# A chunk of attention probabilities turned by DMA instead of TensorE, with all engines in one recorded order

## The chip, the cores and the metric

The kernel runs on 1 core of one Trainium2 chip. The metric is the device time of one execution in microseconds (us). Before the change the median of 3 runs is 3124.31 us (3117.63 to 3127.85).

## What is computed

A decoder trunk of two layers on 2048 tokens of width 1024: a Mamba-2 mixer, then multi-head latent attention with 16 heads, and a final norm. The change lies in the attention between the projections, which is this part of the reference:

```python
MLA_HEADS, QK_NOPE, QK_ROPE, V_HEAD, SEQ, Q_BLOCK = 16, 64, 32, 64, 2048, 128

def causal_block_attention(q_nope, q_rope, k_nope, k_rope, v):
    scale = (QK_NOPE + QK_ROPE) ** -0.5
    for i in range(S // Q_BLOCK):
        q0 = i * Q_BLOCK
        kv_len = q0 + Q_BLOCK
        s = einsum('bqhd,bkhd->bhqk', q_nope[:, q0:kv_len], k_nope[:, :kv_len]) + \
            einsum('bqhr,bkr->bhqk', q_rope[:, q0:kv_len], k_rope[:, :kv_len])
        s = s.astype(float32) * scale
        mask = (q0 + local)[:, None] >= arange(kv_len)[None, :]
        p = softmax(where(mask, s, -inf), axis=-1)
        outs.append(einsum('bhqk,bkhd->bqhd', p, v[:, :kv_len]))
```

## The kernel before

Everything up to the per-head queries, keys and values (the Mamba layer, the norms and projections) and everything after the attention (gate, output projection, final norm) is the same in both kernels. Precision is kept by pairs of float16 halves: a product of two such numbers is three matmuls (lines 86, 87 and 88 in `mm3`), and a float32 tile is split by ScalarE, which writes the high half (L124), and VectorE, which subtracts it and writes the low half (L125), both in `pair16`.

The attention (`heads`) works through 64 jobs, one for each of 16 heads and 4 query blocks of 512 queries. The query block is called qb, 0 to 3; because of the mask, block qb sees qb + 1 chunks of 512 keys. A job has these steps:

- **Scores.** For each of its four rows j of 128 queries and each piece of keys of up to 512: three matmuls into a PSUM bank (and a mask product, L1257, on the last piece), a maximum over the piece by VectorE (L1258), one over the pieces (L1262), then the exponential by ScalarE (L1269) into a float32 tile `Pr`, of which there are 24. `cuts` keeps pieces at 256 keys or more.
- **Turning.** The product with the values needs the probabilities with keys on the partitions. For each block k of 128 keys, TensorE transposes the four 128x128 float32 pieces (L1282) into a PSUM bank `tr`, and `pair16` splits the bank into the float16 tile `PTs`. A job has 4 qb + 4 such units, a head 40 with 136 transposes, as the last four units of a job lie on the diagonal and are narrower.
- **Values.** Two matmuls for each unit (L1292, L1293) add to the job's output bank. After the last unit `finish` copies it out (`Os`, L1299); SyncE's queue stores its upper half to `o_d` and GpSimd's queue adds the lower half to the same place (L1305), which waits for that store to land. After a head's last job the sums of the probabilities are turned and stored (L1308 to L1315).

The order of TensorE's work is written by hand: `LAG`, `DEPTH` and `CREDIT` say after which score piece how many units are turned (T) or multiplied (V). The other engines are ordered by the framework's scheduler. The scores own four PSUM banks (`mm`), turned units and outputs four (`tr`). The next head's queries, keys and values are loaded by GpSimd's queue (L1184 to L1198).

Of the kernel before, what the change touches and what calls it, by code (L numbers as in the profile page):

```python
# [20 lines left out]
P = 128  # L21
# [15 lines left out]
NP = 24  # L37
# [3 lines left out]
LAG = 20  # L41
DEPTH = 2
CREDIT = (
    (("VT",), ("TV",), ("VT",), ("TV",)),
    (("", "VTVT"), ("", "TTVV"), ("", "TTVV"), ("", "TTVV")),
    (("TT", "", "VVTV"), ("TV", "", "VTTV"), ("TV", "", "TTVV"), ("TTV", "", "TVV")),
    (("T", "", "", "VVTTVTV"), ("T", "V", "", "VTTVTV"), ("T", "V", "V", "TVTTV"), ("TV", "V", "", "TVTVT")),
)
KV2, CQ2, GA2, ALL2 = 0, 576, 1344, 3392
MAGIC = 12582912.0  # L50
PSCALE = 32768.0
TINY = 2.0 ** -100
# [14 lines left out]
C1, C2, C3 = 6.28125, 1.93500518798828125e-3, 3.01991598196e-7  # L67


class Net:  # L70
# [374 lines left out]
    def constants(self, cp):  # L445
        nc, a = self.nc, self.a
        self.pack = cp.tile([P, PACK], F32, name="pack")
        self.idb = cp.tile([P, P], BF16, name="idb")

        self.un2, self.unh2 = cp.tile([P, 1], F32, name="un2"), cp.tile([P, 1], F32, name="unh2")  # L450

        self.mk = cp.tile([P, 2 * P], BF16, name="mk")
        at = 0
        for name, n in PACKED:
            setattr(self, name, self.pack[:, at:at + n])
            at += n

    def layer_constants(self, cp):
# [13 lines left out]
        nc.vector.memset(self.mk[:, P:], NEG)  # L472
# [24 lines left out]
        nc.vector.tensor_copy(self.mk[:, 0:P], self.mask)  # L497
# [681 lines left out]
    def load_k(self, h, lo, hi):  # L1179

        nc, ts = self.nc, slice(lo * TB, hi * TB)
        if lo == 0:
            self.keys[h] = self.t(self.hp, "K", [96, 2, T], F16, bufs=2)
        nc.gpsimd.dma_start(self.keys[h][0:64, :, ts], self.kn_d[h * 64:(h + 1) * 64, :, ts])  # L1184
        nc.gpsimd.dma_start(self.keys[h][64:96, :, ts], self.kr_d[:, :, ts])

    def load_v(self, h):

        V = self.vals[h] = self.t(self.xq, "xT", [P, T // P, P], F16, bufs=8)
        self.nc.gpsimd.dma_start(V, self.v_d[:, h * P:(h + 1) * P].rearrange("(k p) d -> p k d", p=P))  # L1190

    def load_q(self, h, n):

        nc, ts = self.nc, slice(n * TB, (n + 1) * TB)
        Q = self.quer[h, n] = self.t(self.xq, "xT", [96, 2, TB], F16, bufs=8)
        nc.gpsimd.dma_start(Q[0:64], self.qn_d[h * 64:(h + 1) * 64, :, ts])
        nc.gpsimd.dma_start(Q[64:80], self.q1_d[h * 16:(h + 1) * 16, :, ts])
        nc.gpsimd.dma_start(Q[80:96], self.q2_d[h * 16:(h + 1) * 16, :, ts])  # L1198
# [7 lines left out]
    def attention(self):  # L1206
        with ExitStack() as ctx:
# [3 lines left out]
            with self.tc.manual_schedule(engines={mybir.EngineType.PE}):  # L1211
                self.heads(sp)

    def heads(self, sp):
        nc, v = self.nc, self.nc.vector
        begun = []
        keys, vals, quer = self.keys, self.vals, self.quer

        def cuts(kv):

            out, at = [], 0
            while at < kv:
                w = min(TB, kv - at)
                if kv - at == TB + P:
                    w = 384
                out.append((at, max(w, 256)))
                at += w
            return out

        def scores(h, qb, st):  # L1230

            if h + 1 < NH:
                if qb == 2:
                    self.load_k(h + 1, 0, NB)
                    self.load_v(h + 1)
                self.load_q(h + 1, qb)
            Q, K = quer.pop((h, qb)), keys[h]
            late = []
            for j in range(4):
                qs = slice(j * P, (j + 1) * P)  # L1240
                parts = cuts(qb * TB + (j + 1) * P)
                nb = len(parts)
                nm = self.t(sp, "nm", [P, 1], bufs=4)
                mx = self.t(sp, "mx", [P, 4], bufs=4) if nb > 1 else nm
                banks = []
                for n, (c0, w) in enumerate(parts):
                    if late:
                        late.pop(0)()
                    begun.append(0)
                    s = self.t(self.pp, "tr" if len(begun) <= 18 and len(begun) % 2 == 1 else "mm", [P, TB], bufs=4)  # L1250
                    ks = slice(c0, c0 + w)
                    self.mm3(s[:, :w], Q[:, 0, qs], Q[:, 1, qs], K[:, 0, ks], K[:, 1, ks], True, n < nb - 1)
                    if n == nb - 1:
                        if qb == j == 0:
                            nc.tensor.matmul(s[:, 0:w], self.idb, self.mk, start=False, stop=True)
                        else:
                            nc.tensor.matmul(s[:, w - P:w], self.idb, self.mk[:, 0:P], start=False, stop=True)  # L1257
                    v.tensor_reduce(mx[:, n:n + 1], s[:, :w], AX.X, ALU.max, negate=nb == 1)  # L1258
                    banks.append((s, w))
                    yield CREDIT[qb][j][n]  # L1260
                if nb > 1:
                    v.tensor_reduce(nm, mx[:, :nb], AX.X, ALU.max, negate=True)  # L1262
                p = {}
                st["P"].append(p)

                def exp(n, at=4 * qb + j, parts=parts, banks=banks, nm=nm, p=p):
                    s, w = banks[n]
# [278 lines left out]
```

## Time and profile before

| what | us |
|---|---|
| median of 3 runs | 3124.31 |
| profiled execution, own time | 3126.91 |
| its span, first to last instruction | 3125.1 |
| VectorE (DVE) busy in the span | 2297.6 |
| ScalarE (ACT) busy | 1963.6 |
| GpSimd (POOL) busy | 609.5 |
| DVE's low halves of turned probabilities (L125, PTs) x640 | 373.1 |
| ACT's exponentials (L1269) x631 | 398.7 |
| TensorE's transposes of probabilities (L1282) x2176 | 318.0 |

Durations of one instruction overlap the next one's on the same engine; what an instruction costs in a busy stretch is the distance from its start to the next start. Matmul ends are modelled, so starts are read for TensorE (PE) too. In the lists of groups a row reads: line, engine, operation, tile written and tiles read, shape, count, then busy us, mean ns of one, idle time of the engine before them and what ended it. In a timeline a row has its start and its length in us; x4 at the end means four in a row. In the waits a row reads: who waited for whom, us in total, times, longest.

### The profile page before, as it was taken

How to read it: one execution, taken by the hardware profiler on the slowest of the kernel's cores; microseconds unless marked ns; L12 is line 12 of the kernel's file. 1: busy time of each engine (PE TensorE's matmuls, PEld its weight loads, DVE VectorE, ACT ScalarE, POOL GpSimd, SP SyncE). 2: the span in 40 equal slices, each digit the busy share in tenths (PEclk: the TensorE clock that was granted, in tenths of full speed). 3: DMA queues.
4: the chain of work that ended last, by engine and by line, in shares of the span. 5: the costliest groups of instructions: out<-in, count | busy, mean ns of one | idle time of the engine just before them, and what ended most of it. 6: DMA issues, size and time to landing. Idle time of an engine off the chain costs nothing.

```text
span 3125.1 us, 50616 instructions
## 1 busy us (share of the span) xinstructions
PE 3033.6 (97%) x17815; PEld 1946.3 (62%) x17815; DVE 2297.6 (74%) x4548; ACT 1963.6 (63%) x4952; POOL 609.5 (20%) x855
## 2 busy tenths in 40 slices
PE   8999999999999999999999999999999999999998
PEld 6777754556556665556665455456666666666687
DVE  6878887788776687776755644468888888888676
ACT  7888576665656465654643433368888888888522
POOL 1222022111221112211111212222222222222100
PEclk9999999999999999999999999999999999999999
DMA  5343667655465454754457556632232323233485
GB/s 179 120 135 107 214 201 256 192 157 179 150 220 179 129 161 128 239 192 129 143 159 270 173 163 202 190 96 55 58 64 55 68 53 66 56 73 89 110 270 163
DMA packets 217138, 456.78 MB, mean 146 GB/s; under 512 B 29154, under 2 KB 71138, under 8 KB 215444
## 3 DMA queue, kind: packets, MB, share of 16 engines
q1 hardware_dynamic: 188980, 375.54, 38.2%
q0 software_dynamic: 27904, 78.02, 9.6%
q8 instruction: 140, 2.29, 0.3%
q14 instruction: 114, 0.93, 0.1%
HBM read 332.21 MB, written 121.25 MB: 145 GB/s over the span
## 4 chain that ended last, share of the span: by engine, by line
PE 52%; issue 10%; DVE 9%; ACT 8%; DMA 5%; POOL 3%; SPq 1%; POOLq 0%; ACTq 0%; DVEq 0%
PE mm L86 10%; PE mm L87 10%; PE mm L88 10%; PE tr L1282 7%; PE tr L1292 3%; PE tr L1293 3%; DVE cacc L691 2%; PE tr L86 1%; PE tr L88 1%; PE tr L87 1%; DMA wraw<-in_ssm_w_in_dram 1%; DMA big<-cumT 1%; PE tr L895 1%; ACT Pr L1269 1%; ACT Xw L888 1%
## 5 line engine op out<-in xcount | busy, mean ns | idle before, releaser
L125 DVE SCALAR_TENSOR_TENSOR PTs<-tr,PTs 128x512 f16<-128x512 f32 (+3 forms) x640 | 373.1, 605 | 96.2 <-ACT PTs L124 90.2
L1269 ACT ACTIVATE Pr<-mm,nm 128x512 f32<-128x512 f32 (+2 forms) x631 | 398.7, 642 | 15.0 <-DVE nm L1262 14.2
L124 ACT ACTIVATE PTs<-tr 128x512 f16<-128x512 f32 (+3 forms) x640 | 331.0, 545 | 115.8 <-PE tr L1282 106.8
L1258 DVE TENSOR_REDUCE mx<-mm 128x1 f32<-128x512 f32 (+2 forms) x569 | 336.1, 615 | 21.0 <-PE mm L88 17.7
L1282 PE MATMUL tr<-pack,Pr 128*128 128x128 f32 x2176 | 318.0, 273 | 2.2 <-ACT Os L1299 2.0
L86 PE MATMUL mm<-xT,wsp 128*128 128x512 f16 (+1 forms) x800 | 308.7, 386 | 0.3 <-ACT wsp L116 0.3
L87 PE MATMUL mm<-xT,wsp 128*128 128x512 f16 (+1 forms) x800 | 306.2, 383 | 0.0
L88 PE MATMUL mm<-xT,wsp 128*128 128x512 f16 (+1 forms) x800 | 304.9, 383 | 0.5 <-DVE wsp L117 0.5
L1282 PEld LDWEIGHTS tr<-pack,Pr 128*128 128x128 f32 x2176 | 253.6, 141 | 69.7 <-ACT Os L1299 2.8
L86 PE MATMUL mm<-wsp,xT 128*128 128x512 f16 (+2 forms) x640 | 233.9, 367 | 6.3 <-ACT craw L685 5.1
L691 DVE SCALAR_TENSOR_TENSOR cacc<-craw,pack,cacc 128x512 f32<-128x512 f32 x288 | 217.1, 773 | 28.4 <-ACT cacc L689 26.6
L87 PE MATMUL mm<-wsp,xT 128*128 128x512 f16 (+2 forms) x640 | 233.4, 365 | 1.4 <-DVE wsp L125 1.3
L88 PE MATMUL mm<-wsp,xT 128*128 128x512 f16 (+2 forms) x640 | 233.0, 365 | 0.0
L86 PE MATMUL mm<-K,xT 96*128 96x512 f16 (+2 forms) x639 | 224.0, 350 | 8.2 <-ACT Pr L1269 6.7
L88 PE MATMUL mm<-K,xT 96*128 96x512 f16 (+2 forms) x639 | 223.0, 349 | 0.0
L87 PE MATMUL mm<-K,xT 96*128 96x512 f16 (+2 forms) x639 | 222.4, 348 | 0.0
L1292 PE MATMUL tr<-PTs,xT 128*128 128x512 f16 (+3 forms) x640 | 221.4, 347 | 0.1
L1293 PE MATMUL tr<-PTs,xT 128*128 128x512 f16 (+3 forms) x640 | 219.5, 347 | 0.0
L86 PE MATMUL mm<-wsp,yT 128*128 128x512 f32 x512 | 210.4, 412 | 1.9 <-DVE sz L721 1.3
L87 PEld LDWEIGHTS <-xT 128*128 128x128 f16 (+1 forms) x1280 | 125.5, 98 | 130.8 <-issue 34.8
L844 POOL TENSOR_TENSOR Xp<-Xw,Xp 128x512 fp32r<-128x512 f32 x64 | 86.6, 1353 | 609.1 <-ACT Xp L843 579.2
L87 PE MATMUL mm<-wsp,yT 128*128 128x512 f32 x512 | 204.2, 399 | 0.0
(457 smaller groups left out, 6965.1 us busy)
## 6 DMA issues: line engine op xcount, KB each, us to landing
wsp<-wo_d SPq DMA_DIRECT2D x96, 512.0 KB, 4.0
wsp<-w_d SPq DMA_DIRECT2D x68, 512.0 KB, 4.4
wraw<-in_ssm_w_in_dram SPq DMA_DIRECT2D x128, 256.0 KB, 3.1
big<-cumT SPq DMA_DIRECT2D x64, 512.0 KB, 4.9
wo_d<-wsp SPq DMA_DIRECT2D x32, 512.0 KB, 3.4
w_d<-wsp SPq DMA_DIRECT2D x32, 512.0 KB, 3.4
st<-w_d SPq DMA_DIRECT2D x56, 256.0 KB, 3.0
wsp<-wu_d SPq DMA_DIRECT2D x28, 512.0 KB, 3.8
```

Of the source, the lines that this page charges most:

```text
L86: mm(out, l_hi, r_hi, start=start, stop=False)
L87: mm(out, l_hi, r_lo, start=False, stop=False)
L88: mm(out, l_lo, r_hi, start=False, stop=stop)
L124: self.nc.scalar.activation(hi, src, AF.Copy, scale=scale)
L125: self.nc.vector.scalar_tensor_tensor(lo, src, scale, hi, ALU.mult, ALU.subtract)
L691: nc.vector.scalar_tensor_tensor(acc, raw[:, k:k + TB], wk[k], acc, ALU.mult, ALU.add)
L844: nc.gpsimd.tensor_tensor(u[:, 1], x, u[:, 0].bitcast(F32), ALU.subtract)
L1258: v.tensor_reduce(mx[:, n:n + 1], s[:, :w], AX.X, ALU.max, negate=nb == 1)
L1269: nc.scalar.activation(x[:, :w], s[:, :w], AF.Exp, bias=nm, accum_out=sums[h][:, at, n:n + 1])
L1282: nc.tensor.transpose(pt[:, j * P:(j + 1) * P], st["P"][j][kb], self.ident)
L1292: nc.tensor.matmul(st["O"][:, c], vals[h][:, kb, :], u[:, 0], start=kb == 0, stop=False)
L1293: nc.tensor.matmul(st["O"][:, c], vals[h][:, kb, :], u[:, 1], start=False, stop=kb == nk - 1)
```

## The change

Five things change, all in the attention.

1. **Chunk 0 of the blocks qb 1, 2 and 3 is turned by DMA** (`TURNED`). For each row j of 128 queries VectorE copies the 128x512 float32 probabilities to float16 (H), GpSimd subtracts (L), and SyncE's queue issues one transposing DMA (X) from this 128x1024 tile `HL` into the tile `PX`, both halves at once. No transpose, ScalarE copy or VectorE subtraction is left for those 12 units of a head. The two matmuls of each unit stay; a job takes these units last. There are 4 `HL` and 2 `PX` tiles.
2. **Pieces of keys** are 512 wide and the last one 128 to 512; the first row of block 0 is 128 wide and no longer 256.
3. **The scale** 32768 goes from the split into the exponent, as an amount added to the maximum (`PSHIFT`): one more small VectorE operation for each row of a job (for block 1 it takes the place of the reduction). The low half is a plain `tensor_tensor`.
4. **Loads of the next head** go from GpSimd's queue to SyncE's, which also has the stores and the X.
5. **The order.** `Pace` plays the 64 jobs through with a fixed time for each step and counts of buffers (8 PSUM banks shared by all, 20 `Pr`), and records every step when it begins; `heads` then writes the instructions of all five engines in that order (`manual_schedule()` without a list of engines). At most 5 score banks are open at once (`SCORED`). It does not model the GpSimd queue's adding store.

```diff
-NP = 24
-LAG = 20
-DEPTH = 2
-CREDIT = (
-    (("VT",), ("TV",), ("VT",), ("TV",)),
...
+BUFS = dict(ps=8, Pr=20, PTs=5, HL=4, PX=2)
+SCORED = 5
+DMA_DELAY = 4000
+TURNED = ((), (0,), (0,), (0,))
+
+def DVE(n):
+    return 62 + n * 1.042, 135
...
+    def tensor(self):
+        f = self.free
+        if self.sums and f["ps"] > 0:
+            return self.rows(self.sums.pop())
+        if self.todo_s and f["ps"] > 0 and self.scored < SCORED:
+            return self.scores(*self.todo_s.pop())
+        if self.todo_t and f["ps"] > 0 and f["PTs"] > 0:
+            n, k = self.todo_t[-1]
+            if all((n, j, k // 4) in self.probs for j in range(self.first(n, k), 4)):
+                return self.turn(*self.todo_t.pop())
+        if self.todo_v and self.todo_v[-1] in self.pairs:
+            if self.todo_v[-1][0] in self.opened or f["ps"] > 0:
+                return self.values(*self.todo_v.pop())
...
+    def high(self, n, j, c):
+        self.give(HL=-1, PX=-((n, c) not in self.dma))
+        self.dma.setdefault((n, c), 4)
+
+        def low():
+            self.issue("POOL", ("L", n, j, c), 1364, 60, moved)
+
+        def moved():
+            self.give(Pr=1)
+            self.queue("SP", 1, lambda: self.issue("SP", ("X", n, j, c), 1300, DMA_DELAY, landed))
...
+        self.issue("DVE", ("H", n, j, c), 345, 130, lambda: self.queue("POOL", 1, low))
...
-            with self.tc.manual_schedule(engines={mybir.EngineType.PE}):
+            with self.tc.manual_schedule():
                 self.heads(sp)
...
+        def N(n, j):
+            qb, m, nm = jobs[n][1], maxima.pop((n, j)), shifts[n, j]
+            if qb == 1:
+                v.tensor_scalar(nm, m[:, 0:1], m[:, 1:2], PSHIFT, ALU.min, ALU.add)
+                return
+            if qb:
+                v.tensor_reduce(nm, m[:, :qb + 1], AX.X, ALU.min)
+            v.tensor_scalar(nm, nm if qb else m[:, 0:1], PSHIFT, None, ALU.add)
...
+        def H(n, j, c):
+            u = halves[n, j, c] = self.t(sp, "HL", [P, 2, TB], F16, bufs=BUFS["HL"])
+            v.tensor_copy(u[:, 0], probs[n, j, c])
+
+        def L(n, j, c):
+            u = halves[n, j, c]
+            nc.gpsimd.tensor_tensor(u[:, 1], probs.pop((n, j, c)), u[:, 0], ALU.subtract)
+
+        def X(n, j, c):
+            if (n, c) not in moved:
+                moved[n, c] = self.t(sp, "PX", [P, 8, TB], F16, bufs=BUFS["PX"])
+            u = halves.pop((n, j, c)).rearrange("p s c -> p (s c)")
+            nc.sync.dma_start(moved[n, c][:, :, j * P:(j + 1) * P], u, transpose=True)
...
+        def B(n, k):
+            pt, tag, c, u = turned[n, k]
+            v.tensor_tensor(u[:, 1, c], pt[:, c], u[:, 0, c], ALU.subtract)
...
+        def O(n):
+            h, qb = jobs[n]
+            o = outs.pop(n)
+            od = self.o_d[h * 64:(h + 1) * 64, qb * TB:(qb + 1) * TB]
+            nc.sync.dma_start(od, o[0:64, :])
+            nc.gpsimd.dma_start(od, o[64:128, :], accum_op=ALU.add)
...
+        steps = dict(S=S, M=M, N=N, E=E, H=H, L=L, X=X, T=T, A=A, B=B, V=V, F=F, O=O, R=R, Y=Y, Z=Z)
+        for what, *where in pace.run():
+            steps[what](*where)
```

**TensorE, units of chunk 0 in the middle of the attention.** Before, the engine turns a unit (four transposes of `Pr` tiles into a bank) and later multiplies its `PTs`:

```order
L1282 MATMUL tr_5439_26899<-pack_66,Pr_5340_26531 128x128
L1282 MATMUL tr_5439_26899<-pack_66,Pr_5354_26583 128x128
L1282 MATMUL tr_5439_26899<-pack_66,Pr_5368_26634 128x128
L1282 MATMUL tr_5439_26899<-pack_66,Pr_5385_26696 128x128
L1282 MATMUL tr_5441_26907<-pack_66,Pr_5344_26548 128x128
L1282 MATMUL tr_5441_26907<-pack_66,Pr_5358_26597 128x128
L1282 MATMUL tr_5441_26907<-pack_66,Pr_5378_26667 128x128
L1282 MATMUL tr_5441_26907<-pack_66,Pr_5386_26698 128x128
L1292 LDWEIGHTS xT_5119_25710
L1292 MATMUL tr_5438_26896<-PTs_5428_26855,xT_5119_25710 128x512
L1293 LDWEIGHTS xT_5119_25710
L1293 MATMUL tr_5438_26896<-PTs_5428_26855,xT_5119_25710 128x512
```

In the change, after the diagonal's last unit (`PTs`, 128 wide) the job's chunk 0 follows from `PX`, between the transposes of the next job:

```order
L1507 LDWEIGHTS xT_4885_24763
L1507 MATMUL tr_5226_26031<-PTs_5268_26170,xT_4885_24763 128x128
L1508 LDWEIGHTS xT_4885_24763
L1508 MATMUL tr_5226_26031<-PTs_5268_26170,xT_4885_24763 128x128
L1507 LDWEIGHTS xT_4885_24763
L1507 MATMUL tr_5226_26031<-PX_5192_25896,xT_4885_24763 128x512
L1508 LDWEIGHTS xT_4885_24763
L1508 MATMUL tr_5226_26031<-PX_5192_25896,xT_4885_24763 128x512
L1481 MATMUL tr_5294_26259<-pack_66,Pr_5169_25809 128x128
L1481 MATMUL tr_5294_26259<-pack_66,Pr_5200_25924 128x128
L1481 MATMUL tr_5294_26259<-pack_66,Pr_5216_25994 128x128
L1481 MATMUL tr_5294_26259<-pack_66,Pr_5245_26091 128x128
```

The multiplications keep their number; the transposes ahead of them are gone for these units.

**VectorE, in the middle of a head.** Before, it holds maxima (`mx`, `nm`) and low halves (`PTs`) alone:

```order
L125 SCALAR_TENSOR_TENSOR PTs_5333_26500<-tr_5332_26495,PTs_5333_26500 128x512
L1258 TENSOR_REDUCE mx_5328_26481<-mm_5334_26503 128x1
L1258 TENSOR_REDUCE mx_5328_26481<-mm_5335_26508 128x1
L1262 TENSOR_REDUCE nm_5327_26480<-mx_5328_26481 128x1
L125 SCALAR_TENSOR_TENSOR PTs_5337_26523<-tr_5336_26518,PTs_5337_26523 128x512
L1258 TENSOR_REDUCE mx_5339_26530<-mm_5341_26533 128x1
```

In the change the copies of chunk 0 (`HL`) stand between them, here the four of one job:

```order
L1465 CAST HL_5500_27017<-Pr_5473_26911 128x512
L1493 TENSOR_TENSOR PTs_5497_27009<-tr_5495_26997,PTs_5497_27009 128x512
L1444 TENSOR_REDUCE mx_5490_26970<-tr_5498_27011 128x1
L1444 TENSOR_REDUCE mx_5490_26970<-mm_5503_27026 128x1
L1465 CAST HL_5507_27046<-Pr_5478_26933 128x512
L1452 TENSOR_REDUCE nm_5489_26969<-mx_5490_26970 128x1
L1453 TENSOR_SCALAR nm_5489_26969<-nm_5489_26969 128x1
L1465 CAST HL_5512_27059<-Pr_5496_27002 128x512
L1465 CAST HL_5515_27067<-Pr_5504_27032 128x512
```

Four copies come in, two of them back to back, and a row's maximum has two small operations where it had one.

**GpSimd, the same job.** Before, this engine issues loads (`xT`) and the adding stores of the outputs (`o_d`):

```order
L1305 DMA o_d_73<-Os_4876_24811 64x512
L1196 DMA xT_4914_24948<-qn_d_75 64x2x512
L1197 DMA xT_4914_24948<-q1_d_76 16x2x512
L1198 DMA xT_4914_24948<-q2_d_77 16x2x512
L1196 DMA xT_4976_25174<-qn_d_75 64x2x512
```

In the change the loads are gone from it, and the subtractions of the low halves stand before and behind the adding stores:

```order
L1469 TENSOR_TENSOR HL_5500_27017<-Pr_5473_26911,HL_5500_27017 128x512
L1540 DMA o_d_73<-Os_5502_27024 64x512
L1469 TENSOR_TENSOR HL_5507_27046<-Pr_5478_26933,HL_5507_27046 128x512
L1469 TENSOR_TENSOR HL_5512_27059<-Pr_5496_27002,HL_5512_27059 128x512
L1469 TENSOR_TENSOR HL_5515_27067<-Pr_5504_27032,HL_5515_27067 128x512
L1540 DMA o_d_73<-Os_5584_27332 64x512
```

Three of this job's four subtractions now stand behind an adding store, which waits for the other half's store to land.

More of the change, by code (lines that the diff above doesn't have):

```diff
@@ L1 @@
+import heapq
 from contextlib import ExitStack
@@ L51 @@
 PSCALE = 32768.0
+PSHIFT = 10.397207708399179
 TINY = 2.0 ** -100
@@ L1324, in ahead @@
                     nc.gpsimd.memset(sums[h], 0.0)
-                yield from scores(h, qb, states[n])
-        units = [(h, qb, kb, states[n]) for n, (h, qb) in enumerate(jobs) for kb in range(4 * qb + 4)]
-        held = []
-        def work(what):
-            if what == "T" and units:
-                a = units.pop(0)
-                held.append((a, turn(*a)))
-            elif what == "V" and held and (len(held) > DEPTH or not units):
-                a, (u, c) = held.pop(0)
-                values(*a, u, c)
```

354 lines of the change are left out of this document (233 added, 121 removed).

## The prediction

> **What bounds the kernel now.** I read the page's busy times first, then the timeline of GpSimd (POOL) for the attention's period, then busy times over one period.
>
> ```profile
> span 3125.1 us, 50616 instructions
> PE 3033.6 (97%) x17815; PEld 1946.3 (62%) x17815; DVE 2297.6 (74%) x4548; ACT 1963.6 (63%) x4952; POOL 609.5 (20%) x855
> ```
>
> ```profile
> 2456.22 0.59 POOL L1196 DMA_DIRECT2D xT<-qn_d  x1 [13.04 <-PE tr L1312]
> ...
> 2510.26 0.59 POOL L1196 DMA_DIRECT2D xT<-qn_d  x1 [13.05 <-PE tr L1312]
> ```
>
> ```profile
> L1282 PE MATMUL tr<-pack,Pr x2176: 269/273/422, 2073.6 to 2936.3; 128*128 128x128 f32 x198
> ```
>
> ```profile
> core 0: us, PE busy (x) PEld busy (x) DVE busy (x) ACT busy (x) POOL busy (x), PEclk, DMA share, GB/s
> 2268.77:2322.81 54.04, 53.80 (x354) 35.50 (x353) 46.33 (x97) 44.82 (x127) 12.29 (x20) 1.00 0.28 59
> ```
>
> The same load returns after 2510.26 - 2456.22 = 54.04 us: that is a head. Sixteen make 865 us, and the transposes run from 2073.6 to 2936.3. In one head TensorE (PE) is busy for 53.80 of 54.04 us at full clock, VectorE (DVE) for 46.33, ScalarE (ACT) for 44.82. The waits of the attention say the same:
>
> ```profile
> POOL o_d L1305 <- DMA o_d<-Os: 86.9, 14, 22.8
> ...
> DVE PTs L125 <- ACT PTs L124: 90.2, 241, 2.5
> ...
> PE mm L86 <- ACT Pr L1269: 6.7, 22, 1.9
> ```
>
> TensorE's matmuls wait for no other engine longer than these 6.7 us in 880, while VectorE waits for ScalarE 241 times. So TensorE sets the time, and work taken from it counts in full until another engine or a wait ends last. Nothing ahead of the attention changes.
>
> **TensorE's part.** Twelve units of a head lose their four transposes.
>
> ```profile
> 2500.18 0.60 PE L1282 MATMUL tr<-pack,Pr 128*128 128x128 f32 x4
> 2500.61 0.38 PE L1292 MATMUL tr<-PTs,xT 128*128 128x512 f16 x1
> ...
> 2503.22 0.27 PE L86 MATMUL mm<-K,xT 96*128 96x256 f16 x1
> 2503.32 0.27 PE L87 MATMUL mm<-K,xT 96*128 96x256 f16 x1
> ```
>
> Four cost 2500.61 - 2500.18 = 0.43 us, so 12 x 0.43 = 5.16 us a head. One row's three score matmuls shrink from 256 keys to 128, about half of 0.10 us each: 0.15 us. TensorE then needs 54.04 - 5.31 = 48.73 us a head; over 16 heads that is **-85.0 us**. The other cuts of keys move columns between pieces and add up to the same.
>
> **VectorE's part.** It loses 12 low halves and gains 12 copies and 12 small operations (one more for each row of blocks 0, 2 and 3).
>
> ```profile
> 2499.50 0.68 DVE L125 SCALAR_TENSOR_TENSOR PTs<-tr,PTs 128x512 f16<-128x512 f32 x1
> 2500.10 0.88 DVE L1258 TENSOR_REDUCE mx<-mm 128x1 f32<-128x384 f32 x2
> ```
>
> ```profile
> L998 DVE CAST sz<-yt 128x512 f32<-128x512 int32 x4 | 1.8, 456 | 4.1 <-DMA yt<-in_positions_dram 4.1
> ...
> L1005 DVE TENSOR_SCALAR sz<-sz 128x512 f32<-128x512 f32 x4 | 1.7, 421 | 0.0
> ```
>
> ```profile
> 2218.09 0.15 DVE L1262 TENSOR_REDUCE nm<-mx 128x1 f32<-128x2 f32 x1
> 2218.21 0.69 DVE L125 SCALAR_TENSOR_TENSOR PTs<-tr,PTs 128x512 f16<-128x512 f32 x1
> ```
>
> A low half costs 0.60 us from start to start: -7.2 us. No row is this copy, float32 to float16 in SBUF. From below it is the 421 ns of the one-input operation less the overlap of 0.08 (0.68 long, 0.60 apart), 0.34; from above the full 0.60 of a two-input one. I take 0.34, as a cast of the same size lasts 456 ns: +4.1 us (7.2 from above). A small operation costs 0.12 us: +1.4 us. VectorE comes to 46.33 - 7.2 + 4.1 + 1.4 = 44.6 us a head, 4.1 us below TensorE's 48.73; with the dear copy 47.7.
>
> **ScalarE's part.**
>
> ```profile
> 2500.88 0.60 ACT L124 ACTIVATE PTs<-tr 128x512 f16<-128x512 f32 x1 [1.52 <-PE tr L1282]
> 2501.37 0.68 ACT L1269 ACTIVATE Pr<-mm,nm 128x512 f32<-128x512 f32 x1
> ```
>
> It loses 12 x 0.49 = 5.9 us and stands at 38.9.
>
> **GpSimd's part and the new wait.** The subtraction's nearest row is one of the same shape:
>
> ```profile
> L844 POOL TENSOR_TENSOR Xp<-Xw,Xp 128x512 fp32r<-128x512 f32 x64 | 86.6, 1353 | 609.1 <-ACT Xp L843 579.2
> ...
> L1305 POOL DMA_DIRECT2D o_d<-Os x64 | 54.1, 846 | 354.1 <-ACT PTs L124 139.3 <-ACT Pr L1269 117.2 <-DMA o_d<-Os 97.6
> ```
>
> ```profile
> L1299 ACT ACTIVATE Os<-tr 128x512 f32<-128x512 f32 x64 | 38.8, 606 | 12.0 <-PE tr L1293 12.0
> ```
>
> ```profile
> o_d<-Os SPq DMA_DIRECT2D x64, 128.0 KB, 2.6
> ```
>
> Twelve subtractions take 16.2 us of a head, so GpSimd has room. But the last product of a job frees both its `PX` tile (so the copies of a later job may start) and its output, whose adding store stands on GpSimd between those subtractions. That store waits for the copy-out (0.61 us) and the landing of the other half (2.6), and takes 0.85 to issue: 4.05 us after the last product, where one copy and one subtraction alone would be through after 0.34 + 1.35 = 1.7. So up to 2.35 us are added for each of three jobs a head. A `Pr` tile is free only after its subtraction; the exponential that takes it next stands in ScalarE's fixed order, behind it the copies of turned units, and behind these TensorE's products. Bounds: 0, if 20 `Pr` tiles and five score banks cover it, and 3 x 2.35 = 7.05 us a head. I take one job in three, 2.35 us: TensorE's wait for exponentials, nearly nothing in the rows, says that most lateness is covered today. **+37.6 us** over 16 heads.
>
> **The lock.** The copies may also meet the subtractions. Before shows VectorE and GpSimd side by side:
>
> ```profile
> 131.14 0.74 DVE L691 SCALAR_TENSOR_TENSOR cacc<-craw,pack,cacc 128x512 f32<-128x512 f32 x1
> 131.81 0.68 DVE L920 TENSOR_TENSOR y<-y,sz 128x512 f32<-128x512 f32 x1
> 132.41 1.77 DVE L691 SCALAR_TENSOR_TENSOR cacc<-craw,pack,cacc 128x512 f32<-128x512 f32 x1
> ```
>
> ```profile
> 131.36 2.27 POOL L844 TENSOR_TENSOR Sp<-st,Sp 128x512 fp32r<-128x512 f32 x1
> ```
>
> GpSimd's subtraction lasts 2.27 us instead of 1.35 while two VectorE operations pass, and then the third lasts 1.77 instead of 0.74: 1.03 us lost. If copies are held as these are, I expect about one of a job's four, 3.1 us a head, inside the margin of 4.1: 0 us. Bounds: 0 and twelve, 12.4 us.
>
> [...]
>
> **DMA and SyncE.** The turn has no row. SyncE's and GpSimd's queues move 256 KB in 3.1 to 5.3 us from issue to landing:
>
> ```profile
> wraw<-in_ssm_w_in_dram SPq DMA_DIRECT2D x128, 256.0 KB, 3.1
> ```
>
> ```profile
> K<-kr_d POOLq DMA_DIRECT2D x14, 256.0 KB, 5.3
> ```
>
> Twelve a head are covered while one in a row costs less than 48.73 / 12 = 4.06 us. I take 3.1, the row of the same queue. The products from `PX` come after a job's other units, and its copies can start two turned jobs earlier, so landing has most of a head's third, some 16 us; the cost is 0. The loads that move to SyncE wait for buffers as they did (13 us at worst in the GpSimd rows) with X and stores behind them; they are needed a head later, and `PX` has that slack. If it is gone, the price is that of rival C. GpSimd is rid of 10 us of issuing a head, which nothing waited for.
>
> **The end.**
>
> ```profile
> L1369 POOL TENSOR_TENSOR K<-wr,K 128x1024 fp32r<-128x1024 f32 x4 | 9.4, 2356 | 14.8 <-ACT K L1368 14.8
> ```
>
> In GpSimd's order two of these stand ahead of the last job's subtractions, after which nothing can fill TensorE: 2 x 2.36 = **+4.7 us**, once (0 if they run before the copies are ready).
>
> **Sum**, against the profiled execution, whose span of 3125.1 us has 1.8 around it: 3126.9 - 85.0 + 37.6 + 4.7 = 3084.2. The median of the runs is 2.6 below that execution: **3082 us**.
>
> **Rivals.**
> A, all covered: 3126.9 - 85.0 + 4.7 - 2.6 = 3044. For it speaks that TensorE hardly waits today; against it that VectorE's margin falls to 4.1 us and that the order is fixed on all engines without the adding store in it.
> B, slower, the lock: each held copy adds 1.03 us, VectorE passes today's 54.04 us once (54.04 - 44.6) / 1.03 = 9.2, so ten of twelve are held. With all: 44.6 + 12.4 = 57.0 us a head, 16 x 2.96 = +47: 3176. Against it: in the rows two VectorE operations pass before GpSimd gets in, and copies often stand back to back. [...]
> C, slower, the GpSimd queue: all three delays reach TensorE, 48.73 + 7.05 = 55.78 us a head, +28: 3157. It turns at 5.31 / 3 = 1.77 us a job. For it: 86.9 us of that wait in 14 times, 6.2 us each, in the rows of before.
> D, about even: two of three delays and some held copies, 53.3 to 54.4 us a head: 3114 to 3135.
> E, the turn is slow: at 5.3 us each in a row, 63.6 us a head, +153: 3282.
> That the transposes don't go is excluded: the built order has them gone.
>
> **How the numbers follow.** Forecast (losses of 1 to 4 us a head, 3058 to 3110) 0.55; A 0.14; D 0.09; C 0.10; B 0.07; E 0.05. A measurement of this kernel can tell about 0.3%, 9.4 us, from no change. Faster by more: 0.55 + 0.14 + 0.03 of D = 0.72; within: 0.05 of D; slower: 0.10 + 0.07 + 0.05 + 0.01 = 0.23. The range goes from just under A, 3040, to C's end, 3155: it leaves out E, most of B and the fast edge of A, 0.05 + 0.06 + 0.04, and what lies above C, 0.04.
>
> **What would show it.** 1408 transposes; a period of 51.1 us a head. The copy near 0.42 us long where nothing holds it, and about 1.4 where it is held; more than four long ones in twelve would overdraw VectorE's margin. Waits of exponentials for subtractions, one cluster a head, and adding stores waiting for the other half, behind them late subtractions. If TensorE waits at products from `PX`, the turn is late and E or C is at work; if its busy share stays at 99%, A is. The forecast is wrong if the new order alone leaves TensorE idle where no copy, subtraction or turn is near.

## The result and the profile after

The changed kernel takes **3237.05 us** (median of 4 runs, 3234.82 to 3242.90) against 3124.76 for the kernel before on the same chip: a ratio of 1.0366, 95% interval 1.0343 to 1.0389. It is slower by 112 us, above the predicted range of 3040 to 3155. The profiled execution took 3242.9 us. One execution of the last experiment, `add_hact_free`, took 5026 us at a granted clock of 0.557 and is left out of its median and ratio.

The page of the changed kernel, then the busy times over thirteen heads of its attention (from the turning of one head's row sums to that of the thirteenth after it):

```profile
span 3241.0 us, 49983 instructions
...
PE 3004.5 (93%) x17047; PEld 1876.4 (58%) x17047; DVE 2324.8 (72%) x4739; ACT 1882.4 (58%) x4760; POOL 699.0 (22%) x822
```

```profile
core 0: us, PE busy (x) PEld busy (x) DVE busy (x) ACT busy (x) POOL busy (x), PEclk, DMA share, GB/s
...
2111.00:2905.80 794.80, 673.15 (x3953) 401.77 (x3952) 613.25 (x1391) 516.15 (x1467) 224.88 (x221) 0.94 0.58 105
```

The row sums are turned once a head, so their first and last start give the mean period of the changed kernel:

```profile
L1526 PEld LDWEIGHTS tr<-pack,ri x16: 87/88/133, 2110.6 to 3041.7; 128*16 128x16 f32 x16
```

(3041.7 - 2110.6) / 15 = 62.07 us a head, 54.04 before, 48.73 by TensorE's work alone. Over the thirteen heads the period is 794.8 / 13 = 61.1 us. In it TensorE is busy for 673.15 / 13 = 51.8 us and idle for 9.4, and its granted clock has fallen from 1.00 to 0.94. VectorE is busy for 47.2 us and ScalarE for 39.7 (predicted 44.6 and 38.9): no engine is full. The time goes into waits. Those of the attention on which the argument rests (who waited for whom, us in total, times, longest):

```profile
POOL o_d L1540 <- DMA o_d<-Os: 140.6, 30, 8.8
...
ACT Pr L1459 <- POOL HL L1469: 90.3, 36, 9.5
...
PE mm L279 <- ACT Pr L1459: 67.8, 56, 8.7
...
PE tr L1526 <- DVE nm L1453: 53.2, 14, 12.7
...
PE tr L1481 <- ACT Pr L1459: 16.7, 7, 4.0
```

Before, TensorE's matmuls waited 6.7 us for exponentials; now 67.8 + 16.7 = 84.5. Exponentials wait for GpSimd's subtractions, which no trace of before has. The fourth row is new too: TensorE waits 53.2 us to turn the row sums. It is put down to the last VectorE operation ahead; what the transpose reads is written by L1522, and that operation, 0.26 us in the mean before, lasts 1.67 here (columns: count, busy us, mean ns of one, idle time before):

```profile
L1469 POOL TENSOR_TENSOR HL<-Pr,HL 128x512 f16<-128x512 f32 x192 | 236.0, 1368 | 320.6 <-ACT Os L1515 123.3 <-ACT PTs L1488 76.7 <-DVE nm L1452 58.5
...
L1465 DVE CAST HL<-Pr 128x512 f16<-128x512 f32 x192 | 107.8, 598 | 17.0 <-DMA PX<-HL 15.3 <-issue 1.5
...
L1522 DVE TENSOR_SCALAR ri<-ri 128x16 f32<-128x16 f32 x16 | 26.7, 1670 | 0.5
```

```profile
PX<-HL SPq DMA_TRANSPOSE x192, 3.2
```

One such stall of the changed kernel, all engines in order of time (SPq is SyncE's queue issuing a DMA):

```profile
2482.58 0.63 ACT L1515 ACTIVATE Os<-tr 128x512 f32<-128x512 f32 x1
...
2483.46 4.05 SPq L1389 DMA_DIRECT2D xT<-qn_d  x1
...
2488.89 0.91 SPq L1539 DMA_DIRECT2D o_d<-Os  x1
...
2492.18 0.83 POOL L1540 DMA_DIRECT2D o_d<-Os  x1 [8.17 <-DMA o_d<-Os]
2492.76 3.64 POOL L1469 TENSOR_TENSOR HL<-Pr,HL 128x512 f16<-128x512 f32 x3
2494.22 0.69 ACT L1459 ACTIVATE Pr<-mm,nm 128x512 f32<-128x512 f32 x1 [8.92 <-POOL HL L1469]
...
2495.05 0.58 PE L279 MATMUL mm<-K,xT 96*128 96x512 f16 x1 [8.07 <-ACT Pr L1459]
```

Read it from the bottom. TensorE stands for 8.07 us, since an exponential stands for 8.92, since the `Pr` tile that it takes is freed by a subtraction, since that subtraction is behind the adding store on GpSimd, which waits 8.17 us for the other half of its job. That half was copied out from 2482.58 on but its store issued only at 2488.89: on SyncE's queue it was behind a query load whose issue lasted 4.05 us instead of 0.58, and the load's two other parts. The busy times around the stall show the second price:

```profile
2487.00:2491.00 4.00, 0.00 (x0) 0.00 (x0) 0.00 (x0) 0.00 (x0) 0.00 (x0) 0.93 1.08 190
2491.00:2495.00 4.00, 0.00 (x0) 0.00 (x0) 0.00 (x0) 0.78 (x3) 2.82 (x4) 0.50 0.63 101
2495.00:2499.00 4.00, 3.95 (x13) 2.37 (x13) 1.72 (x3) 2.11 (x7) 1.40 (x2) 0.50 0.92 175
2499.00:2503.00 4.00, 4.00 (x21) 2.14 (x20) 3.09 (x8) 2.82 (x9) 0.00 (x0) 0.79 0.12 22
2503.00:2507.00 4.00, 4.00 (x25) 2.32 (x24) 3.75 (x9) 3.41 (x12) 0.00 (x0) 1.00 0.15 49
```

In 2487 to 2491 no engine computes. TensorE's clock falls to 0.50 for the last 4 x (1.00 - 0.93) / 0.50 = 0.6 us of these, some 3.4 us after its last matmul, and it stays there when the work returns at 2495.05, through the next row and for 4 x (1.00 - 0.79) / 0.50 = 1.7 us of the one behind it, to about 2500.7. That is 2495 to 2500.7 at half speed: 4 x 0.50 + 4 x 0.21 = 2.8 us more. In this stall, then, 3.4 us without work lie before the fall and 5.6 us of work, 2495.05 to about 2500.7, before the rise; what sets these two moments isn't shown.

### The profile page after: what moved, and what is told of

It reads as the page before. It is cut to its first block, busy times and chain, and to the rows that moved or that the text cites. A ratio compares the mean times of both kernels' runs of the same rounds, so it can differ in the third digit from the quotient of the medians.

```text
span 3241.0 us, 49983 instructions
## 1 busy us (share of the span) xinstructions
PE 3004.5 (93%) x17047; PEld 1876.4 (58%) x17047; DVE 2324.8 (72%) x4739; ACT 1882.4 (58%) x4760; POOL 699.0 (22%) x822
## 5 line engine op out<-in xcount | busy, mean ns | idle before, releaser
L1459 ACT ACTIVATE Pr<-mm,nm 128x512 f32<-128x512 f32 (+3 forms) x522 | 324.0, 629 | 95.2 <-POOL HL L1469 61.5
L1444 DVE TENSOR_REDUCE mx<-mm 128x1 f32<-128x512 f32 (+3 forms) x522 | 308.4, 602 | 72.7 <-PE mm L281 50.0
L1493 DVE TENSOR_TENSOR PTs<-tr,PTs 128x512 f16<-128x512 f32 (+2 forms) x447 | 251.8, 570 | 113.6 <-ACT PTs L1488 110.2
L1469 POOL TENSOR_TENSOR HL<-Pr,HL 128x512 f16<-128x512 f32 x192 | 236.0, 1368 | 320.6 <-ACT Os L1515 123.3
L1488 ACT ACTIVATE PTs<-tr 128x512 f16<-128x512 f32 (+2 forms) x447 | 221.1, 509 | 139.1 <-PE tr L1481 136.8
L1481 PE MATMUL tr<-pack,Pr 128*128 128x128 f32 x1407 | 235.2, 288 | 32.7 <-ACT Pr L1459 16.7
L279 PE MATMUL mm<-K,xT 96*128 96x512 f16 (+4 forms) x530 | 192.8, 364 | 69.0 <-ACT Pr L1459 67.8
L280 PEld LDWEIGHTS <-xT 128*128 128x128 f16 (+1 forms) x1280 | 127.4, 100 | 187.1 <-issue 101.9
L279 PE MATMUL mm<-wsp,yT 128*128 128x512 f32 x512 | 210.2, 411 | 3.1 <-DMA wsp<-wo_d 2.0
L280 PE MATMUL mm<-wsp,yT 128*128 128x512 f32 x512 | 204.3, 399 | 0.0
L281 PE MATMUL mm<-wsp,yT 128*128 128x512 f32 x512 | 203.7, 399 | 0.0
L281 PEld LDWEIGHTS <-xT 128*128 128x128 f16 (+1 forms) x1280 | 126.5, 99 | 123.6 <-issue 12.7
L1064 ACT ACTIVATE big<-big,d_cum 128x128 f32<-128x128 f32 x512 | 168.1, 391 | 48.7 <-DMA big<-cumT 48.6
```

Of the source, the lines that this page charges most:

```text
L279: mm(out, l_hi, r_hi, start=start, stop=False)
L280: mm(out, l_hi, r_lo, start=False, stop=False)
L281: mm(out, l_lo, r_hi, start=False, stop=stop)
L1064: act(E[:, h, :], E[:, h, :], AF.Relu, bias=ncum[:, h0 + h:h0 + h + 1])
L1444: v.tensor_reduce(maxima[n, j][:, c:c + 1], s[:, :w], AX.X, ALU.max, negate=True)
L1459: nc.scalar.activation(x[:, :w], s[:, :w], AF.Exp, bias=shifts[n, j], accum_out=sums[h][:, 4 * qb + j, c:c + 1])
```

## The experiments

All times are medians of 4 to 10 runs (3 for `add_hact_free`); the kernel before took 3125 to 3130 us beside them. The **theory** after the trace: the adding store's place among the subtractions (theory 1), with TensorE's wait for the row sums (theory 2) beside it. The **rivals**: the recorded order costs by itself (theory 3), or VectorE's copies, locked by subtractions, do. A plan (`Pace`) that gets another time for one step writes all engines in another order; "the same order" below means that every engine's other instructions stay where they were.

**The order alone** (`order_only`).

```diff
-TURNED = ((), (0,), (0,), (0,))
+TURNED = ((), (), (), ())
```

> TURNED is empty: the timed order on all engines, the new pieces of keys, the shift in the exponent and the loads on SyncE's queue stay, all 640 units are turned by TensorE again (2176 transposes), no copy, subtraction or turn by DMA is left. Theory 1 (the adding store on GpSimd holds up the subtractions behind it, these the exponentials, these TensorE) and theory 2 (the sums' scaling held by subtractions): nothing stands behind the adding store and nothing locks VectorE, so TensorE's need of before less 0.15 us a head, 54.04 - 0.15, is the period: 3120 to 3135 us, granted clock near 1.00. Theory 3 (the recorded order itself leaves TensorE idle): 3200 us or more, with TensorE waiting for exponentials as in the changed kernel.

Measured 3174.41 us, ratio 1.0150 (1.0126 to 1.0173): 48 us slower than before, though nothing is turned by DMA. It lies between the theories. This plan has other work to order, so its order is not that of the changed kernel to the letter. Its row sums, and TensorE in one head:

```profile
L1526 PE MATMUL mm<-pack,ri x3: 269/273/273, 2338.0 to 2452.6; 128*16 128x128 f32 x3
```

```profile
2340.00:2397.20 57.20, 54.50 (x354) 34.66 (x352) 46.71 (x107) 45.59 (x124) 3.43 (x5) 1.00 0.29 56
```

The period is (2452.6 - 2338.0) / 2 = 57.3 us against 54.04, at full clock, with short waits only (2.2 us at the longest in the list, and 9.8 us in all of score matmuls for exponentials, against 67.8). So theory 3 is right that the order has a price, and wrong about the wait behind it. Which of the parts that stay (the order, the pieces of keys, the shift, the loads) costs it wasn't tried, and how much of it the changed kernel pays isn't shown.

**The adding store** (`no_add` leaves it out, `add_late` moves it, both in the same order otherwise).

```diff
+ADD_LATE = 8000
...
             self.order.append(("O", n))
+            self.at(self.now + ADD_LATE, lambda: self.order.append(("G", n)))
...
-            nc.gpsimd.dma_start(od, o[64:128, :], accum_op=ALU.add)
...
+        def G(n):
+            h, qb = jobs[n]
+            od = self.o_d[h * 64:(h + 1) * 64, qb * TB:(qb + 1) * TB]
+            nc.gpsimd.dma_start(od, outs.pop(n)[64:128, :], accum_op=ALU.add)
```

> The adding store of the lower half on GpSimd's queue is left out (the output lacks that half), nothing else changes. Theory 1: the 84.5 us that TensorE waits for exponentials in the rows (67.8 at scores, 16.7 at transposes) go nearly all, and with the long gaps most of the time at the halved clock (TensorE is busy 3.4 us a head longer than its 48.73): 3237 - 84 - 40 = 3113, range 3090 to 3150. Theory 3 (order) or the lock alone: no subtraction gets through earlier than its copy lets it, 3220 to 3240. In every theory TensorE's wait for the row sums (53 us) stays.

> The adding store is recorded 8 us of planned time after the store of the other half, so that the subtractions of the next copies stand ahead of it; nothing is left out. Theory 1: as without the adding store, within 15 us of that run, 3100 to 3150, and GpSimd's idle time before its adding stores no longer ends at the landing of the other half. A rival to theory 1, that the adding store's transfer and not its place costs the time (DMA engines, writes to the same rows): the time stays near 3237 here though it falls without the adding store.

Measured 3124.50 without it (ratio 0.9992, 0.9978 to 1.0005) and 3123.93 moved (0.9994, 0.9984 to 1.0005). Both win 113 us, and the same, so it is the store's place and not its transfer. The waits with the store moved (line numbers are larger by 2, L1548 is the store), and the busy times over twelve heads:

```profile
PE tr L1483 <- DVE PTs L1495: 34.0, 16, 3.8
...
PE mm L281 <- ACT Pr L1461: 22.6, 45, 2.0
PE tr L1528 <- DVE nm L1455: 22.1, 14, 7.4
...
POOL o_d L1548 <- DMA o_d<-Os: 18.3, 3, 8.5
...
ACT Pr L1461 <- POOL HL L1471: 9.2, 21, 0.8
```

```profile
2108.10:2749.90 641.80, 588.79 (x3642) 356.86 (x3640) 575.96 (x1284) 477.39 (x1355) 213.98 (x204) 0.99 0.66 118
```

The wait for the landing falls from 140.6 us to 18.3, that of exponentials for subtractions from 90.3 to 9.2 with no long one left, and even the row sums' wait more than halves. TensorE is busy for 588.79 / 12 = 49.1 us a head where it was for 51.8. Theory 1 is shown, at 113 us in this order. An estimate of what these consist of: all of TensorE's waits in the two lists fall by 73 us (154.7 to 82.1), and its busy time by 16 x (51.8 - 49.1) = 43, as its clock stays up (0.99 for 0.94). What TensorE waits for longest now is VectorE's low halves, 34.0 us (15.5 in the changed kernel).

**The row sums** (`sums_late` gives the plan a later turning, `sums_free` takes the held operation out in the same order).

```diff
-                self.queue("DVE", 3, lambda: self.issue("DVE", ("R", n), 600, 130, summed))
+                self.queue("DVE", 3, lambda: self.issue("DVE", ("R", n), 600, 7000, summed))
```

```diff
-            v.tensor_scalar(ri, ri, 0.5 * PSCALE, None, ALU.mult)
...
-            nc.scalar.activation(r, ps[:16, 0:P], AF.Copy)
+            nc.scalar.activation(r, ps[:16, 0:P], AF.Copy, scale=0.5 * PSCALE)
```

> The plan lets TensorE turn the row sums 7 us after VectorE has them (130 ns in the changed kernel), so that other work of TensorE stands ahead of that transpose; the adding store stays where it is. Theory 2: the 53 us in 14 waits of TensorE at that transpose go: 3237 - 53 = 3184 (3170 to 3200). Rival: TensorE is ahead of the exponentials there anyway and waits for them a little later: under 20 us are won, 3217 to 3237, and the waits for exponentials grow by what the sums' wait loses.

> Both repairs at once: the adding store recorded 8 us late, the row sums turned 7 us late. If the two causes are separate, what TensorE still waits for the row sums with the late adding store (22 us in 14 waits) goes: 3124 - 22 = 3102, range 3085 to 3115. If the gains of the two runs add up in full, 3237 - 113 - 72 = 3052. If another wait takes their place: 3115 to 3130.

> The changed kernel, order to the letter, but VectorE's scaling of the reciprocal row sums (the operation that lasted 1.67 us in the mean and up to 4.87 beside subtractions, 0.26 before the change) is left out, and ScalarE applies the factor in the copy of the turned sums that it makes anyway. Theory 2, TensorE's 53 us at the row sums are a cost by themselves: 3237 - 53 = 3184, range 3170 to 3200. Rival, the exponentials behind the adding store end last anyway: 3215 to 3240.

> The adding store 8 us late and VectorE's scaling of the row sums left out, as in the run before. The row sums' remaining wait of 22 us goes: 3124 - 22 = 3102, range 3092 to 3112. If something else ends last there: 3115 to 3128.

Measured: `sums_late` 3164.75, but `add_sums_late` 3162.34, where 3102 was expected and the adding store alone had given 3124. `sums_late` looked like a win of 72 us for theory 2; the second run says that it was another plan, in which the adding store's place hardly matters (2 us), so that something else must end last. In the same order the edit is worth 4.5 us (`sums_free`, 3232.57; 11 by the ratios to the kernel before, whose intervals overlap) and 9 with the store moved (`add_sums_free`, 3114.96; ratio 0.9952, 0.9937 to 0.9967). In `sums_free` the row sums are turned in L1525. TensorE's wait there falls from 53.2 to 16.7 us, and its waits for exponentials rise from 84.5 to 74.7 + 42.2 = 116.9:

```profile
ACT Pr L1459 <- POOL HL L1469: 123.0, 37, 9.3
...
PE mm L279 <- ACT Pr L1459: 74.7, 54, 8.4
...
PE tr L1481 <- ACT Pr L1459: 42.2, 7, 6.8
...
PE tr L1525 <- DVE nm L1453: 16.7, 7, 3.4
```

So 36.5 us less at the row sums came back as 32.4 more at exponentials. Theory 2 falls as a cause of its own, as long as the chain behind the adding store ends last. With the store moved the wait falls from 22.1 to 14.6 us, and at least these 7.5 are won.

**SyncE's queue** (`kv_pool`: keys and values loaded by GpSimd's queue again).

```diff
-                        self.load_k(h + 1, 0, NB, nc.sync)
-                        self.load_v(h + 1, nc.sync)
+                        self.load_k(h + 1, 0, NB)
+                        self.load_v(h + 1)
```

> The changed kernel with only the next head's keys and values loaded by GpSimd's queue again (queries stay on SyncE's). Theory of SyncE's queue: the store that the adding store waits for is late since it stands behind a query load whose issue lasts 4 us right after the load of the values; with keys and values elsewhere that store is issued on time, the longest waits of TensorE (5 to 8.7 us once in each two heads) go, and with them the halved clock behind them: 3160 to 3185. Rival: GpSimd's loads stand ahead of subtractions and hold them as long: 3225 or more. Rival: the landing itself is slow, with keys and values in the same DMA engines: within 10 us of 3237.

Measured 3267.36 (ratio 1.0423, 1.0395 to 1.0450), 30 us worse, in the range of the first rival. That the loads hold subtractions is not shown as the reason: copies wait 73.2 us for turns there, 15.3 in the changed kernel. In this head of its trace the query load is short, and the X ahead of the store has the long issue:

```profile
2496.97 6.04 SPq L1475 DMA_TRANSPOSE PX<-HL  x1
2503.10 0.57 SPq L1389 DMA_DIRECT2D xT<-qn_d  x1
...
2505.05 0.57 SPq L1539 DMA_DIRECT2D o_d<-Os  x1
```

So the query load isn't slow in itself. In the changed kernel the one right behind the load of the values takes 1.3 to 4.5 us to issue in each of 14 heads; here, with that load on GpSimd's queue, it takes 0.57, and the X ahead of it 6.04. Why is open.

**The copies' lock.** `h_act` lets the plan put the copies on ScalarE; `act_oldplan` keeps the order and changes only the engine; `dve_newplan` takes the plan for ScalarE and leaves the copies on VectorE.

```diff
-                self.queue("DVE", 3, lambda: self.high(n, j, c),
+                self.queue("ACT", 3, lambda: self.high(n, j, c),
...
-        self.issue("DVE", ("H", n, j, c), 345, 130, lambda: self.queue("POOL", 1, low))
+        self.issue("ACT", ("H", n, j, c), 490, 160, lambda: self.queue("POOL", 1, low))
...
-            v.tensor_copy(u[:, 0], probs[n, j, c])
+            nc.scalar.activation(u[:, 0], probs[n, j, c], AF.Copy)
```

> As with both repairs, and ScalarE instead of VectorE makes the copy to float16 (H), with the plan's time for it set to 490 ns. Lock theory: the copies on VectorE take 0.8 us in the mean beside GpSimd's subtractions instead of 0.42, some 5 us of VectorE a head, and the delays behind them are what keeps the period at 52 to 54 us; on ScalarE nothing holds them: 30 to 60 us faster than with both repairs. Order theory: the recorded order alone costs 3 us a head (54.05 against 57.2 without any turning) whatever engine copies: within 15 us of the run with both repairs.

> The changed kernel with the copies on ScalarE (plan: 490 ns) and nothing else; the adding store stays ahead of subtractions. If the lock and the adding store are separate costs that add up: 3237 less the 70 us that the copies on ScalarE won when both repairs were in, 3165, range 3145 to 3185. If the adding store is the last wait wherever it stands: 3215 to 3240, and TensorE's waits for exponentials stay above 60 us. In both, VectorE's scaling of the row sums can still be held by a subtraction.

> The adding store recorded 8 us late and the copies on ScalarE, the row sums as in the changed kernel. Lock theory: 3124 (adding store late, copies on VectorE) less some 5 us of held copies a head less what ScalarE's 5.9 us more costs: 3045 to 3085. Rival, the plan with copies on VectorE and the row sums in their old place had room for held copies: within 12 us of 3124. The row sums' wait of 22 us may stay here.

> The changed kernel's recorded order to the letter; only the engine that executes the copies changes, from VectorE to ScalarE. Lock theory: the copies are no longer held, so most of the 133 us come: 3095 to 3140. Plan theory (the order made for copies on ScalarE is the better one, the lock is small): 3200 to 3240. If it is both: between.

> The order that the plan makes for copies on ScalarE, but VectorE executes the copies. Lock theory: they are held as in the changed kernel: 3200 to 3240. Plan theory: 3100 to 3130, as with copies on ScalarE.

> The changed kernel's order with copies executed by ScalarE and the adding store recorded 8 us late. Against the run with copies on ScalarE alone in this order it gives the price of the adding store's place when no copy is held. One chain (a held copy makes subtractions late, and the adding store does the rest): under 35 us are won. Two separate costs: 80 to 113 us are won, as with copies on VectorE.

| order of | copies on | store as changed | store 8 us late |
|---|---|---|---|
| the changed kernel | VectorE | 3237.05 | 3123.93 |
| the changed kernel | ScalarE | 3250.35 | 3160.29 |
| the plan for ScalarE | VectorE | 3189.98 | not run |
| the plan for ScalarE | ScalarE | 3104.00 | 3081.86 |

(`late_hact`, with the row sums late as well, 3092.14.) After the first two runs the lock looked like the cause, with 133 us. The cross of order and engine speaks against so simple a reading: in the unchanged order, copies that no subtraction holds win nothing (13 us worse, 36 worse with the store late). ScalarE pays for them there, with 0.64 us each or 7.6 us a head, so the lock isn't ruled out. The order alone wins 47 us with VectorE's copies (3190 against 3237), and another 86 come only when engine and plan agree. The adding store costs 113 and 90 us in the changed kernel's order but 22 in the plan for ScalarE. That would fit an order with more room ahead of the exponentials, which covers the same late subtraction; it isn't shown. The lock's own price is not separated by these runs. What it does on VectorE is seen with the store late:

```profile
L1467 DVE CAST HL<-Pr 128x512 f16<-128x512 f32 x192 | 149.7, 821 | 1.7 <-issue 1.5
```

Twelve copies of 0.82 us instead of 0.42 are 4.8 us of VectorE a head, more than the predicted margin of 4.1, and busy times over 700 us of attention (sums; with the store late, then with copies on ScalarE as well) show VectorE at 90% and at 78%:

```profile
sum 700.00, PE 643.32 PEld 390.46 DVE 629.83 ACT 521.18 POOL 231.65; mean PE 91.90 PEld 55.78 DVE 89.97 ACT 74.45 POOL 33.09
```

```profile
sum 700.00, PE 670.50 PEld 405.78 DVE 546.13 ACT 616.40 POOL 230.39; mean PE 95.79 PEld 57.97 DVE 78.02 ACT 88.06 POOL 32.91
```

**The last two heads** (`TURN_HEADS = 14`: heads 14 and 15 are turned by TensorE).

```diff
-            here = [t for t in tiles if t[1] // 4 not in turned[qb]]
+            here = [t for t in tiles if h >= TURN_HEADS or t[1] // 4 not in turned[qb]]
...
-            if c in self.turned[self.jobs[n][1]]:
+            if self.jobs[n][0] < TURN_HEADS and c in self.turned[self.jobs[n][1]]:
```

> As with both repairs, but heads 14 and 15 are turned by TensorE as before the change (136 transposes each). The last two heads take 61.7 and 63.9 us where the others take 53; theory: the output weights' splits (2.4 us each, eight on GpSimd) stand among these heads' subtractions. Without subtractions there the two heads cost 10.6 us of TensorE more and lose some 19 us of waits: 0 to 15 us faster than with both repairs. If the splits cost by themselves, on whatever engine they hold: 5 to 15 us slower.

> As with the adding store late and copies on ScalarE, with heads 14 and 15 turned by TensorE. As with copies on VectorE (3162 to 3148) some 15 us are won: 3030 to 3070. If ScalarE, which also makes the high halves of the output weights there, was what held the last heads: within 6 us of the run without it.

> The adding store late, the row sums turned late, copies on ScalarE, heads 14 and 15 turned by TensorE: 3092 - 15 = 3077, range 3062 to 3088. Against the run with the row sums in their old place it shows what the sums' delay does when nothing holds VectorE's copies: if the sums' wait is a cost by itself this is the faster one by 10 to 25 us, if the delay only shifts the plan it is not.

Measured 3147.63 against 3162.34 (15 us won), 3086.47 against 3081.86 and 3090.36 against 3092.14 (nothing won). The end of `add_late` shows what is there: the row sums of its last four heads, and the splits of the output weights on GpSimd (here L1574):

```profile
L1528 PE MATMUL tr<-pack,ri x4: 269/271/372, 2749.9 to 2928.0; 128*16 128x128 f32 x4
```

```profile
L1574 POOL TENSOR_TENSOR W<-wr,W x4: 2337/2345/2354, 2824.6 to 2865.9; 128x1024 fp32r<-128x1024 f32 x4
L1574 POOL TENSOR_TENSOR K<-wr,K x4: 2350/2530/2602, 2853.0 to 2915.7; 128x1024 fp32r<-128x1024 f32 x4
```

```profile
L1528 PE MATMUL tr<-pack,ri x16: 269/269/372, 2108.1 to 2928.0; 128*16 128x128 f32 x16
```

The first twelve periods are (2749.9 - 2108.1) / 12 = 53.5 us, the last three together 178.1, 17.7 us more. All eight splits lie there, and ScalarE's parts of them. That they alone cost these 17.7 us isn't shown, since leaving the turning out beside them won time in one of three orders.

**The best version.** `add_hact`, 3081.86 us, is faster than both kernels: ratio to before 0.9852 (0.9824 to 0.9880).

> The adding store late, copies on ScalarE in the plan made for it, VectorE's scaling of the row sums left out. TensorE waits there for the sums for under 6 us in all before this edit, so it stays within 8 us of 3082: 3074 to 3086. If it gains more, the held scaling cost VectorE's later work.

Without VectorE's scaling of the row sums as well, `add_hact_free` measured 3076.76 (3075.26 to 3082.93), ratio 0.9837 (0.9821 to 0.9854): within the 8 us that were expected, and not clear of noise. The change's idea, then, is worth some 46 us here, with the adding store away from the subtractions and the copies where the plan has them.

## Why the prediction was wrong

**What held.** All 1408 transposes are in the trace (1407 in the row of the `tr` banks, one in an `mm` bank). TensorE's need fits (49.1 us a head with the store moved, for 48.73), ScalarE's busy time too (39.7 for 38.9), the subtraction lasts 1.37 us, the free copy 0.42, and the turn lands in 3.2 us where 3.1 was taken. No product waits for `PX`, so rival E is out.

**The step that failed: "the late subtractions behind the adding store".** The mechanism was the right one, link by link, and rival C named it. The size was wrong twice. The delay was priced at 2.35 us a job, from a landing of 2.6 us right after the copy-out; the rows have 30 landing waits of 140.6 us, 4.7 in the mean and 8.8 at the longest. The landing itself is as forecast:

```profile
o_d<-Os SPq DMA_DIRECT2D x64, 128.0 KB, 2.4
```

What is late is its start: in some 20 of the 64 jobs SyncE's queue issues the store 3 us or more after the copy-out, up to 6.3, as in the stall above, where loads stand ahead of it. The prediction saw loads and X ahead of the stores and gave them no cost. And the share that reaches TensorE was taken as one in three, +37.6 us, because TensorE hardly waited before. The runs give **113 us**. That this is also 16 x 7.05, the upper bound, is chance: the bound has 48 delays of 2.35 us at full clock, and the runs have fewer and longer ones, with a slower clock behind them. That TensorE had room in the old order says nothing of the new one, as the table of orders and engines shows.

**The new order was costed at nothing.** `order_only` gives it 48 us without any turning. The prediction took 48.73 us a head as reached, by the sum of TensorE's work; the text named this as what would make it wrong, and gave it neither a term nor a rival.

**The lock.** Taken at 0 with one of four copies held by 1.03 us, 3.1 us a head. Measured in the changed kernel: (598 - 419) x 12 = 2.1 us a head over the median, and the scaling of the row sums, which had no term, takes 1.67 - 0.26 = 1.4 us more. VectorE comes to 47.2 us a head and not to 44.6, which leaves 1.5 of the margin of 4.1. As a loss of its own the lock didn't show in the changed kernel's order. With the store moved it is 4.8 us. That it then costs TensorE time is likely from VectorE's 90% and from the 34.0 us that TensorE waits for low halves; with copies on ScalarE these are 22.7 in the same order (`act_oldplan_late`) and 1.6 in `add_hact`. But neither run came with that gain alone, so it isn't shown.

**The end.** +4.7 us was taken for two splits of the output weights; eight stand among the last heads' subtractions, and with the store moved these heads take 17.7 us more.

**The clock** had no term. The stall shown costs 2.8 us more through it. Over all heads TensorE's longer busy time is the estimate of 43 us above, which lies inside the 113.

Does it add up? From rival A's 3044 to 3237 are 193 us. The store's place is 113, the row sums 9, the order 48 if it costs the same with turning, the end 17.7 - 4.7 = 13: 183. That is a fit and no proof, since the order's share was measured without turning, the lock has no share in it, and the shares are not independent. Of the 80 us by which the kernel with the store moved (3124) stays above rival A, only the 9 of the row sums were won by a run in the same order. (By its own 53.3 us a head rival D starts at 3117 and not at 3114; nothing rests on it.)

## What to carry to other kernels

An instruction that waits for a DMA, put on an engine's queue ahead of work that others need, can cost the whole landing and whatever that transfer's own queue adds (here 2.4 us and up to 6.3): price it from the queue it is issued on, and give it a place in the order of its own, behind the work. A new order written for all engines has a price of its own, which a run of the order with the old work in it shows at once. And a wait's total in the list is not what its removal wins: here 36.5 us less at one line were worth 4.5, since the chain behind the adding store took the rest back.

## What the hardware showed

The copy and the scaling of the changed kernel, with their shortest, median and longest ns:

```profile
L1465 DVE CAST HL<-Pr x192: 408/419/5926, 2068.0 to 3035.5; 128x512 f16<-128x512 f32 x192
```

```profile
L1522 DVE TENSOR_SCALAR ri<-ri x16: 160/1292/4866, 2109.0 to 3040.3; 128x16 f32<-128x16 f32 x16
```

The longest scaling and the longest copy, and what GpSimd did beside them:

```profile
2840.66 4.87 DVE L1522 TENSOR_SCALAR ri<-ri 128x16 f32<-128x16 f32 x1
```

```profile
2840.76 4.72 POOL L1469 TENSOR_TENSOR HL<-Pr,HL 128x512 f16<-128x512 f32 x4
```

```profile
2960.09 5.93 DVE L1465 CAST HL<-Pr 128x512 f16<-128x512 f32 x1
```

```profile
2958.51 2.54 POOL L1469 TENSOR_TENSOR HL<-Pr,HL 128x512 f16<-128x512 f32 x2
2960.74 0.40 POOL L1425 MEMSET sum<- 128x64 f32 x1
2960.84 4.88 POOL L1568 TENSOR_TENSOR K<-wr,K 128x1024 fp32r<-128x1024 f32 x2
```

Eight of the 16 scalings, of 16 elements a partition, have no GpSimd instruction beside them and last 0.16 to 0.17 us. The longest ends 0.05 us after four subtractions in a row. The longest copy, which meets the second of two subtractions, ends 0.3 us after the two splits of the output weights that follow. In neither row does VectorE's operation end between the GpSimd instructions, and of the copies and scalings that have a row of the timeline to themselves all 19 over 0.5 us stand beside a subtraction, while those without a GpSimd instruction beside them last 0.43 us at most. What holds them is in no row.
